# The last tokens' output projection in a two-layer diffusion step: its non-attention half moved into the first score block

## The chip, the cores and the metric

One Trainium2 chip, one core. The metric is the device time of one execution in microseconds (us): the median of three runs of the kernel before is 3267.5 us (3267.45 to 3268.93). TensorE (PE) multiplies, with its weight loads shown apart (PEld); VectorE (DVE), ScalarE (ACT) and GpSimd (POOL) work on tiles; SyncE (SP) issues all the DMAs of this kernel, in program order. Each engine runs its own instructions in order.

## The reference, cut to what matters

```python
D_MODEL, SEQ, DEPTH, DEC_SEQ, PAST_LEN, N_HEADS, N_KV_HEADS = 1024, 256, 2, 2048, 256, 8, 2

def _layer(x, mod, norm_g, w_in, q_g, k_g, conv_w, conv_b, pool_w, pool_scale, w_out, angs, ctx_k, ctx_v):
    shift, scl, gate = jnp.split(mod, 3, axis=-1)
    xn = _rmsnorm(x, norm_g) * (1 + scl) + shift
    proj = xn @ w_in
    q, k, v, z_a, h_c, b_c, c_c, z_c, u_p, z_p = jnp.split(proj, SPLIT_IDX, axis=-1)
    ...                                               # norms and rotary positions of q and k
    attn = _attend(q, k_all, v_all) * jax.nn.silu(z_a)            # channels 0 to 511
    conv = b_c * _short_conv(c_c * h_c, conv_w, conv_b) * jax.nn.silu(z_c)    # 512 to 767
    pool = _pool_mix(u_p, pool_w, pool_scale) * jax.nn.silu(z_p)              # 768 to 1023
    out = jnp.concatenate([attn, conv, pool], axis=-1) @ w_out
    return x + gate * out, k, v
```

It runs for 256 prompt tokens (which attend to themselves) and for 2048 sample tokens (which attend to themselves and to 256 cached keys), in two layers. After the second layer every token is normalized (`_rmsnorm(z, final_g)`). All is float32; the kernel splits each float32 operand of a product into a high and a low part and adds three products (high by high, high by low, low by high).

## The kernel before

Each layer has two phases. Phase A (`phase_a`) normalizes, transposes and multiplies by `w_in`; it writes q, k, v and the gates to DRAM, and the conv and pool channels, already final, as `mH` and `mL` (high and low parts, four chunks of 128 channels). Phase B (`phase_b`) does the attention and the output projection. The order of execution is phase A of layer 0, phase B of layer 0, then the same for layer 1.

Phase B walks over 292 steps. A unit is one head of one block of 512 sample tokens (nine steps of 256 keys), or one pair of prompt heads (one step). Blocks 0 to 3 have eight units each; block 0 also has the four prompt units, one after each of its first four heads. Block 3, the last tokens, takes its heads in the order 4 to 7, 0 to 3 (`h ^ 4 if B.tail`), so that pair 1 ends last. A step s issues on PE the four score products of its 256 keys (`qk`), the value products of a step three earlier (`pv`, LAG = 3), and about two pieces of a coming unit's row maximum (`max_pieces`); ACT takes two exponentials, POOL the low part `pl`, DVE the sums `Z` and the maxima. With a unit's last step come the products of its nine low parts, `fin_a` (adding the two halves), `fin_b`, `fin_b2` (the reciprocal of the sum) and, with the second head of a pair, `fin_c` (c1 to c4: scale, gate on POOL, high part on ACT, low part on POOL), which leaves the pair's tiles in `B.mix`.

The output projection is cut into small functions that wait in a list, `fill`; every step runs one of them (`fill.run`). For blocks 0 to 2 and for the prompt, `outproj` is put there some steps after the block's last pair: 64 functions of six products of 256 columns. In layer 1 the norm of these rows follows, in the list `slow`: `fin_load` reads half a row tile back from DRAM into one of two buffers `oy`, ACT scales it, POOL multiplies by `final_g`, SP writes it out.

Block 3 has no later steps to hide in. Its projection (`outproj_tail`) takes 384 products of 256 columns: per tile of 128 tokens and 256 output columns, 12 for the non-attention channels and 12 for the attention channels. Six of the 16 tiles are begun ahead (`ahead`), the first six functions from five steps before the last step (`el`), the others after the last step; the rest follows in `rest`. Five steps before the end `fill.flush()` empties the list, so that block 2's projection is issued, and `early` loads the conv and pool channels, weights and x. `add` adds products to x and, in layer 1, squares; `finish` takes the root by Newton steps (`newton`, 12 small DVE instructions), scales and writes. `beside` holds the norms of phase A's first two blocks of layer 1, run inside `finish` of layer 0.

Two structures matter for the order: `at(s, f)` puts a function on a step; and a buffer with a fixed count (`bufs`) makes the SP instruction that refills it wait for its last reader, with all that stands behind it on SP.

Of the kernel before, what the change touches and what calls it, by code (L numbers as in the profile page):

```python
# [19 lines left out]
D = 1024  # L20
# [11 lines left out]
PR = {'po': 6, 'q1': 3, 'q2': 5, 's0': 14, 's0p': 7, 'q1p': 2, 'ma': 3, 'mb': 1, 'd0': 3, 'd1': 2, 'dp': 1,  # L32
# [63 lines left out]
def hybrid_step(ctx: ExitStack, tc: tile.TileContext, A, O):  # L96
# [45 lines left out]
    xP2 = scratch("xP2", [NP, D], F32)  # L142

# [889 lines left out]
    def phase_b(l, xs_src, xp_src, xs_dst, xp_dst, nxt):  # L1033
# [3 lines left out]
        with ExitStack() as st, ExitStack() as left:  # L1037
# [6 lines left out]
            def kv_tiles(prompt):  # L1044
                if prompt:
                    t = wk.tile([128, 4, 512], F32R, tag="cl", name="kvp", bufs=1)
                    for g in range(2):
                        for a, v in zip(kvs[True], (t[:, g, 0:256], t[0:65, g, 256:512], t[:, 2 + g, 0:128]
                                                    .bitcast(F16).rearrange("p (t e) -> p t e", e=128))):
                            a.append(v)  # L1050
                    return
# [155 lines left out]
            def zsum(u, grp, ns):  # L1207
# [4 lines left out]
                def one(i):  # L1212
# [48 lines left out]
            def fin_b(u, bc):  # L1261
                ps = pmx.tile([128, 4, 2], F32, tag="mx", name="lc")
                for q in range(4):
                    for i, z in enumerate(u.z2 if u.fh else u.z):
                        nc.tensor.matmul(out=ps[:, q, :], lhsT=z[:, q * 128:(q + 1) * 128], rhs=vones_h if u.fh else vones, start=(i == 0),
                                         stop=(i == u.fh))
# [13 lines left out]
            def fin_c(zs, o, bc, B, pair):  # L1280

                n = B.n
                st = {}

# [6 lines left out]
                def c2():  # L1291
                    padd(o[:, 0:n], o[:, 0:n], zs[:, 0:n], ALU.mult)
# [17 lines left out]
            def outproj(B):  # L1310
# [68 lines left out]
                if last:  # L1379
# [38 lines left out]
                    for t in range(nt):  # L1418
# [6 lines left out]

            def outproj_tail(B):


                rows = [slice(B.t0 + t * 128, B.t0 + (t + 1) * 128) for t in range(4)]
# [3 lines left out]
                def load_x(t, tag, n, bufs):  # L1433
                    xs[t] = []
                    for i in range(0, D, n):
                        x = wk.tile([128, n], F32, tag=tag, name="ox", bufs=bufs)
                        nc.sync.dma_start(out=x, in_=xs_src[rows[t], i:i + n])
                        xs[t] += [x[:, k:k + 512] for k in range(0, n, 512)]

                def load_w(c, part, tile, k0):  # L1440

                    n = tile.shape[1]
                    load(tile, (woH, woL)[part][l][0][:, k0:k0 + n, c * 256:(c + 1) * 256])
                    for k in range(n):
                        ws[c, part, k0 + k] = tile[:, k, :]

                def early():
                    state["c"] = []
                    for i, (tag, m) in enumerate((("ch", mH), ("cl", mL))):
                        t = wk.tile([128, 4, 512], F32R, tag=tag, name=tag, bufs=1)  # L1450
                        load(t, m[:, :, B.t0:B.t0 + 512])
                        state["c"].append(t)
                        for k0 in (4, 0):
                            load_w(1 + i, 1 - i, wk.tile([128, 4, 256], F32R, tag="wo", name="wo", bufs=4), k0)
                    load_x(0, "ox", D, 2)
# [297 lines left out]
```

## Time and profile before

| | |
|---|---|
| median of three runs | 3267.5 us |
| the profiled execution | 3276.25 us, span 3274.5 us |
| phase B, steps 0 to 291 | 709 to 1599 us in layer 0, 2288 to 3200 us in layer 1 |
| PE busy | 3091.0 us, 94% |
| DVE, POOL, ACT busy | 2305.9, 2042.5, 1836.5 us |

A busy time is the share in which the profile shows an instruction running. PE's products overlap, so the distance from one start to the next tells what a product costs, not its length. PEclk is the granted clock of PE as a share of full speed: 1.0 is 2.4 GHz, 0.5 is 1.2 GHz. In the timelines a line has the start in us, the length in us, the engine, the line, the operation, out<-in, shape and count (runs of the same instruction are merged); in brackets the idle time of the engine before it and what ended it.

### The profile page before, as it was taken

How to read it: one execution, taken by the hardware profiler on the slowest of the kernel's cores; microseconds unless marked ns; L12 is line 12 of the kernel's file. 1: busy time of each engine (PE TensorE's matmuls, PEld its weight loads, DVE VectorE, ACT ScalarE, POOL GpSimd, SP SyncE). 2: the span in 40 equal slices, each digit the busy share in tenths (PEclk: the TensorE clock that was granted, in tenths of full speed). 3: DMA queues.
4: the chain of work that ended last, by engine and by line, in shares of the span. 5: the costliest groups of instructions: out<-in, count | busy, mean ns of one | idle time of the engine just before them, and what ended most of it. 6: DMA issues, size and time to landing. Idle time of an engine off the chain costs nothing. (4 is left out here: it accounts for less than half of the span.)

```text
span 3274.5 us, 48199 instructions
## 1 busy us (share of the span) xinstructions
PE 3091.0 (94%) x17818; PEld 2450.8 (75%) x17818; DVE 2305.9 (70%) x3720; ACT 1836.5 (56%) x2638; POOL 2042.5 (62%) x1312
## 2 busy tenths in 40 slices
PE   7899999998999999999999999999899999999997
PEld 5788888765677777767789877987557776676776
DVE  5655575368888888888568546834888888788774
ACT  3223342148877777777533224322888777787772
POOL 2424363238888888887543344521788888798884
PEclk9999999999999999999999999999999999999998
DMA  7245744361341323143633454433323424243335
GB/s 245 74 141 184 246 136 136 117 156 31 94 150 54 103 78 103 52 127 95 207 118 97 142 188 164 144 101 95 73 70 115 127 76 135 64 133 89 102 125 199
DMA packets 367011, 400.02 MB, mean 122 GB/s; under 512 B 31028, under 2 KB 317240, under 8 KB 366008
## 3 DMA queue, kind: packets, MB, share of 16 engines
q1 hardware_dynamic: 366776, 396.94, 39.3%
q8 instruction: 142, 2.33, 0.3%
q14 instruction: 93, 0.76, 0.1%
HBM read 281.50 MB, written 115.36 MB: 121 GB/s over the span
## 5 line engine op out<-in xcount | busy, mean ns | idle before, releaser
L180 POOL TENSOR_TENSOR pl<-P,ph 128x1024 f16<-128x1024 f32 (+2 forms) x594 | 1235.1, 2090 | 277.7 <-ACT ph L1197 260.7
L1147 DVE TENSOR_REDUCE mr<-mx 128x1 f32<-128x512 f32 x1024 | 695.4, 685 | 292.3 <-PE mx L1146 287.1
L1195 ACT ACTIVATE P<-st 128x1024 f32<-128x1024 f32 x576 | 636.6, 1105 | 295.5 <-PE st L1186 287.3
L1217 DVE TENSOR_REDUCE Z<-P 128x152 f32<-128x912 f32 (+2 forms) x576 | 696.1, 1209 | 6.6 <-ACT P L1195 5.5
L1197 ACT ACTIVATE ph<-st 128x1024 f16<-128x1024 f32 x584 | 592.3, 1014 | 0.0
L1146 PE MATMUL mx<-KH,T 128*128 128x512 f32 x1024 | 488.0, 478 | 34.5 <-DVE mr L1147 21.7
L634 PE MATMUL rest<-xh,wh 128*128 128x512 f32 (+1 forms) x1264 | 479.0, 379 | 12.3 <-ACT wh L425 8.6
L636 PE MATMUL rest<-xh,wl 128*128 128x512 f32 (+1 forms) x1264 | 470.0, 372 | 6.2 <-DVE wl L427 4.4
L635 PE MATMUL rest<-xl,wh 128*128 128x512 f32 (+1 forms) x1264 | 469.9, 372 | 0.0
L1185 PE MATMUL st<-T,KH 128*128 128x512 f32 x1152 | 462.8, 402 | 3.1 <-ACT ph L1197 3.1
L1186 PE MATMUL st<-T,KL 65*128 65x512 f32 x1152 | 460.5, 400 | 0.0
L1231 PE MATMUL pv<-ph,V 128*128 128x512 f16 x1152 | 353.9, 389 | 7.7 <-ACT P L1195 4.5
L1146 PEld LDWEIGHTS mx<-KH,T 128*128 128x128 f32 x1024 | 195.7, 191 | 195.3 <-DVE mr L1147 87.1
L634 PEld LDWEIGHTS rest<-xh,wh 128*128 128x128 f32 x1264 | 242.1, 192 | 55.9 <-ACT wh L425 8.8
L427 POOL TENSOR_TENSOR wl<-wf,wh 128x512 fp32r<-128x512 f32 x88 | 124.6, 1416 | 254.5 <-ACT wh L425 230.6
L636 PEld LDWEIGHTS rest<-xh,wl 128*128 128x128 f32 x1264 | 241.5, 191 | 48.7 <-DVE wl L427 5.7
L635 PEld LDWEIGHTS rest<-xl,wh 128*128 128x128 f32 x1264 | 242.2, 192 | 36.9
L1186 PEld LDWEIGHTS st<-T,KL 65*128 65x128 f32 x1152 | 219.4, 190 | 48.1
L1185 PEld LDWEIGHTS st<-T,KH 128*128 128x128 f32 x1152 | 220.1, 191 | 42.8 <-ACT ph L1197 6.1
L475 PE MATMUL qkv<-wl,xh 128*128 128x256 f32 x864 | 247.1, 286 | 4.3 <-DVE wl L427 2.8
L474 PE MATMUL qkv<-wh,xh 128*128 128x256 f32 x864 | 250.9, 290 | 0.0
L476 PE MATMUL qkv<-wh,xl 128*128 128x256 f32 x864 | 246.3, 285 | 0.0
(241 smaller groups left out, 5638.8 us busy)
## 6 DMA issues: line engine op xcount, KB each, us to landing
wo<-woH SPq DMA_DIRECT2D x68, 512.0 KB
wo<-woL SPq DMA_DIRECT2D x68, 512.0 KB
wf<-in_w_in SPq DMA_DIRECT2D x50, 512.0 KB
wa<-in_w_ada SPq DMA_DIRECT2D x24, 1024.0 KB
wf<-in_w_in SPq DMA_DIRECT2D x19, 1024.0 KB
woH<-wgh SPq DMA_DIRECT2D x64, 256.0 KB
woL<-wgl SPq DMA_DIRECT2D x64, 256.0 KB
T<-qH SPq DMA_DIRECT2D x128, 128.0 KB
```

The costliest lines, as they stand in the source:

```text
L180: nc.gpsimd.tensor_tensor(out=out, in0=a, in1=b, op=op)
L634: nc.tensor.matmul(out=ps[:, 0:b.n], lhsT=wh[:, k, ms], rhs=b.h[:, k, :], start=(k == 0), stop=False)
L635: nc.tensor.matmul(out=ps[:, 0:b.n], lhsT=wh[:, k, ms], rhs=b.l[:, k, :], start=False, stop=False)
L636: nc.tensor.matmul(out=ps[:, 0:b.n], lhsT=wl[:, k, ms], rhs=b.h[:, k, :], start=False, stop=(k == KD - 1))
L1146: nc.tensor.matmul(out=ps, lhsT=u.T1[:, q * 128:(q + 1) * 128], rhs=u.KH[u.g][:, c * 512:(c + 1) * 512])
L1147: nc.vector.reduce_max(out=mr[:, q, c:c + 1], in_=ps, axis=AX.X)
L1185: nc.tensor.matmul(out=ps[:, i, :], lhsT=u.KH[u.g][:, kt], rhs=u.T1, start=True, stop=False)
L1186: nc.tensor.matmul(out=ps[:, i, :], lhsT=u.KL[u.g][0:65, kt], rhs=u.T2, start=False, stop=True)
L1195: nc.scalar.activation(out=P, in_=ps, func=AF.Exp, scale=0.125)
L1197: nc.scalar.activation(out=ph, in_=ps, func=AF.Exp, scale=0.125)
L1217: nc.vector.tensor_reduce(out=z[:, c], in_=u.P[grp][:, 0:ns, c, :].rearrange("p s n t -> p n s t"), axis=AX.XY, op=ALU.add)
L1231: nc.tensor.matmul(out=u.po, lhsT=u.V[u.g][:, 2 * j + i, :], rhs=ph[:, i, :], start=(j == 0 and i == 0), stop=False)
```

## The change

In each layer:

- At step 6 a new function list, `outproj_ahead`, is put into `fill` for block 3's tokens: the 192 products of the non-attention channels, in 32 functions of six products, with loads of `mH`, `mL`, weights and x, the sum x + products being written to a new DRAM tensor `xT`. It stands in block 0, where `fill` was empty until the prompt's projection.
- `outproj_tail` keeps the attention channels alone, 96 products of 512 columns, one PSUM tile of 1024 columns per row tile. Five half tiles of them take pairs 2, 3 and 0 in `ahead`, one function per step from the last step on; pair 1 and all else is in `rest`.
- The tail's weights go to `KH1`, `KL1` (22 and 16 steps before the end) and `ch`, `cl` (5 steps before); x comes from `xT`, tiles 2 and 3 ten steps before the end, tiles 0 and 1 five steps before.
- For the last pair, c2 and c4 run on DVE in place of POOL, and the last sum of `Z` is no longer added on POOL: `fin_b` takes two `Z` tiles (twice the small products).
- In layer 1, block 2's rows are read back whole, into the four `wo` tiles, five steps before the end (`late_loads`), and scaled and multiplied as whole rows (`late`). The tail's rows 0 and 1 share one Newton root; the product with `final_g` of half of each row is on DVE (`scalar_tensor_tensor`), the other half on POOL.
- The loop ends as soon as nothing is pending, and phase A's first loads of layer 1 are then issued ahead of `rest`. `fill` runs one function at a time in the tail.
- The prompt's tiles `kvp` and `Pp` get space of their own (one `Pp` buffer, not one of four `wo`).

```diff
-                    t = wk.tile([128, 4, 512], F32R, tag="cl", name="kvp", bufs=1)
+                    t = kvp.tile([128, 2, 640], F32R, tag="kvp", name="kvp")
-                    u.P[0] = wk.tile([128, 1, 512, 2], F32, tag="wo", name="Pp", bufs=4)
+                    u.P[0] = wk.tile([128, 1, 512, 2], F32, tag="Pp", name="Pp", bufs=1)
-                        if grp and (u.blk or grp == 1 or not PR['zl']):
+                        if grp and not (u is units[-1] and grp == u.nst // GRP - 1):
                             padd(z, z, u.z.pop())
+                sub = dsub if B.tail and pair == 1 else padd
...
-                    padd(lo[:, 0:n], o[:, 0:n], h[:, 0:n], ALU.subtract)
+                    sub(lo[:, 0:n], o[:, 0:n], h[:, 0:n], ALU.subtract)
...
+                    def late_loads():
+                        for t in range(nt):
+                            y = wk.tile([128, D], F32, tag="wo", name="oy", bufs=4)
+                            state["y", t] = y
+                            nc.sync.dma_start(out=y, in_=dst[r0:r0 + 128, :])
+                    def late(t, part):
+                        if part == 0:
+                            nc.scalar.mul(out=y, in_=y, mul=state["r"][:, t:t + 1])
+                        else:
+                            padd(y, y, fg, ALU.mult)
+                            nc.sync.dma_start(out=out[r0:r0 + 128, :], in_=y)
...
+            def outproj_ahead(B):
+                def load_c(c):
+                    for w in (woH, woL):
+                        t = wk.tile([128, 4, 256], F32R, tag="wo", name="wo", bufs=4)
+                        load(t, w[l][0][:, 4:8, cs])
+                    x = wk.tile([128, 4, 256], F32, tag="ox", name="ox", bufs=2)
+                    nc.sync.dma_start(out=x, in_=xs_src[rows, cs].rearrange("(t p) n -> p t n", p=128))
+                def start():
+                    for tag, m in (("ch", mH), ("cl", mL)):
+                        load(t, m[:, :, rows])
+                    load_c(0)
+                def mm(c, t, q):
+                    if (t, q) == (0, 1) and c < 3:
+                        load_c(c + 1)
...
+                    if q:
+                        nc.vector.tensor_tensor(out=x[:, t], in0=x[:, t], in1=ps, op=ALU.add)
+                        if t == 3:
+                            nc.sync.dma_start(out=xT[l][:, c * 256:(c + 1) * 256].rearrange("(t p) n -> p t n", p=128),
+                                              in_=x)
+                return ([start, lambda: None, lambda: None]
+                        + [lambda c=c, t=t, q=q: mm(c, t, q) for c in range(4) for t in range(4) for q in range(2)])
...
+                def end():
+                    for part in range(2):
+                        load_w(1, part)
+                    for t in range(2):
+                        xs[t] = wk.tile([128, D], F32, tag="ox", name="ox", bufs=2)
+                        nc.sync.dma_start(out=xs[t], in_=xT[l][t * 128:(t + 1) * 128, :])
...
+                def add(t):
+                    for a, p in ([(x, ps[t])] if t in ps else [(x[:, c], ps[t, c]) for c in range(2)]):
+                        nc.vector.tensor_tensor(out=a, in0=a, in1=p, op=ALU.add)
+                    if last:
+                        for c in range(2):
+                            nc.scalar.activation(out=j, in_=x[:, c], func=AF.Square, accum_out=state["ss"][:, t, c:c + 1])
+                        padd(x[:, 1], x[:, 1], fg[:, 512:1024], ALU.mult)
+                def finish(ts):
+                        r = newton(sm, s, e - a, "or", EPS)
+                    for t in ts:
+                            nc.vector.scalar_tensor_tensor(out=x[:, 0:512], in0=x[:, 0:512], scalar=rt, in1=fg[:, 0:512],
+                                                           op0=ALU.mult, op1=ALU.mult)
+                            nc.scalar.mul(out=x[:, 512:1024], in_=x[:, 512:1024], mul=rt)
+                        nc.sync.dma_start(out=y[B.t0 + t * 128:B.t0 + (t + 1) * 128, :], in_=x)
+                    if beside and ts[-1]:
                         beside.pop(0)()
+                ahead = [lambda: mm(2, 0, (2, 3, 0)), lambda: mm(0, 0, (2, 3, 0)), lambda: mm(0, 1, (2, 3, 0)),
+                         *[lambda c=c, k=k: mm(1, c, (k,)) for c in range(2) for k in (2, 3, 0)]]
+                rest = [lambda: mm(0, 0, (1,)), lambda: mm(0, 1, (1,)), lambda: add(0),
+                        lambda: mm(1, 0, (1,)), lambda: mm(1, 1, (1,)), lambda: add(1), lambda: finish((0, 1)),
+                        lambda: mm(2, 0, (1,)), lambda: mm(2, 1, (2, 3, 0, 1)), lambda: add(2), lambda: finish((2,)),
+                        lambda: mm(3, 0, (2, 3, 0, 1)), lambda: mm(3, 1, (2, 3, 0, 1)), lambda: add(3), lambda: finish((3,))]
+            at(PR['oa'], lambda: fill.add(outproj_ahead(B)))
...
                     fill.flush()
-                    tail[0]()
-                    fill.add([lambda: None] * PR['gap'] + tail[5][:6])
+                    tail[1]()
+                    if last:
+                        before_last.loads()
+                if s >= NSTEP and not (pvq or zq or soon or todo or first):
+                    break
+                if s >= NSTEP - 1 and tail[2]:
+                    fill.add([tail[2].pop(0)])
...
-                nf = 2 if NSTEP - 60 < s < NSTEP and s % PR['fx'] == 0 or s >= NSTEP + 3 else 1
+                nf = 2 if NSTEP - 60 < s < NSTEP and s % PR['fx'] == 0 else 1
...
                 left.close()
-                tail[7].extend(next(nxt))
+                tail[4].extend(next(nxt))
+            fill.add(tail[2] + tail[3])
             while fill.q:
-                fill.run(2)
-                due += 2 * rate
+                fill.run()
+                due += rate
```

## Rows read from the trace of the kernel before

**Rows 1.** The page: busy time of each engine, share of the span, instructions.
```profile
PE 3091.0 (94%) x17818; PEld 2450.8 (75%) x17818; DVE 2305.9 (70%) x3720; ACT 1836.5 (56%) x2638; POOL 2042.5 (62%) x1312
```

**Rows 2.** Stretches: block 0 of both layers, block 1 of layer 0, both tails.
```profile
core 0: us, PE busy (x) PEld busy (x) DVE busy (x) ACT busy (x) POOL busy (x), PEclk, DMA share, GB/s
732.00:833.00 101.00, 87.37 (x421) 53.36 (x420) 83.06 (x118) 82.61 (x117) 82.21 (x47) 0.98 0.19 56
2310.00:2414.00 104.00, 91.87 (x423) 57.09 (x423) 84.30 (x119) 82.70 (x117) 82.37 (x47) 0.94 0.20 60
1012.00:1104.00 92.00, 90.63 (x522) 69.53 (x521) 77.59 (x109) 70.28 (x85) 77.05 (x42) 1.00 0.32 92
...
1598.00:1657.00 59.00, 55.68 (x437) 51.66 (x436) 23.19 (x54) 13.64 (x23) 10.10 (x10) 0.94 0.73 256
3199.00:3257.00 58.00, 54.35 (x426) 50.47 (x424) 23.11 (x56) 13.98 (x26) 26.50 (x34) 0.94 0.62 213
```

**Rows 3.** Timeline of PE: products of 256 and of 512 columns, back to back.
```profile
3216.08 0.28 PE L1493 MATMUL op<-wt,ch 128*128 128x256 f32 x1
3216.20 0.28 PE L1494 MATMUL op<-wt,ch 128*128 128x256 f32 x1
...
3102.40 0.40 PE L1186 MATMUL st<-T,KL 65*128 65x512 f32 x1
3102.64 0.40 PE L1185 MATMUL st<-T,KH 128*128 128x512 f32 x1
```

**Rows 4.** Timeline of the last head of layer 1, from its last score product.
```profile
3199.10 0.61 PE L1231 MATMUL pv<-ph,V 128*128 128x512 f16 x2
...
3204.75 0.58 PE L1495 MATMUL op<-wt,cl 128*128 128x256 f32 x1 [3.65 <-DMA cl<-mL]
...
3206.78 3.70 PE L1238 MATMUL pv<-pl,V 128*64 128x512 f16 x18
...
3212.67 0.95 PE L1265 MATMUL lc<-vones,Z 128*128 128x2 f32 x8
...
3217.53 0.69 DVE L1289 TENSOR_TENSOR o<-o,rlb 128x512 f32<-128x512 f32 x1 [3.69 <-PE rlb L1288]
...
3220.32 1.29 POOL L180 TENSOR_TENSOR mixl<-o,mixh 128x512 fp32r<-128x512 f32 x1 [0.30 <-ACT mixh L1296]
```

**Rows 5.** Timeline of layer 0's end: last head, phase A's loads, squares, norms.
```profile
1619.25 1.29 POOL L180 TENSOR_TENSOR mixl<-o,mixh 128x512 fp32r<-128x512 f32 x1 [0.73 <-ACT mixh L1296]
...
1626.95 4.00 SPq L299 DMA_DIRECT2D x<-xS  x8
...
1630.79 1.06 ACT L312 ACTIVATE junk<-x 128x1024 bf16<-128x1024 f32 x1 [11.62 <-DMA x<-xS]
...
1635.87 0.17 DVE L316 TENSOR_SCALAR ms<-ss 128x4 f32<-128x4 f32 x1 [2.17 <-ACT junk L312]
...
1638.47 2.74 DVE L323 TENSOR_SCALAR x<-x,nt_y 128x1024 f32<-128x1024 f32 x4
...
1656.73 1.52 DVE L441 TENSOR_SCALAR xf<-trx,modA,modB 128x512 f32<-128x512 f32 x2
```

**Rows 6.** Waits of 3199 to 3274 us: engine, line, releaser, us in total, times, longest.
```profile
ACT oy L1412 <- DMA oy<-xS: 12.8, 4, 5.3
```

**Rows 7.** Timeline of layer 1's end: a Newton step beside POOL, adds, squares, last scaling.
```profile
3256.90 1.26 POOL L180 TENSOR_TENSOR ox<-ox,fg 128x512 f32<-128x512 f32 x1
3256.99 1.18 DVE L151 TENSOR_TENSOR nt_t<-nt_t,nt_v 128x1 f32<-128x1 f32 x1
...
3260.04 1.28 DVE L1502 TENSOR_TENSOR ox<-ox,op 128x512 f32<-128x512 f32 x2
...
3265.49 0.63 ACT L1505 ACTIVATE oj<-ox 128x512 bf16<-128x512 f32 x1
3266.03 0.19 ACT L1505 ACTIVATION_READ_ACCUMULATOR oj<-ox 128x1 f32 x1
...
3270.15 0.72 ACT L1519 ACTIVATE ox<-ox,nt_y 128x512 f32<-128x512 f32 x1 [3.94 <-DVE nt_y L152]
```

More of the change, by code (lines that the diff above doesn't have):

```diff
@@ L142, in hybrid_step @@
     xP2 = scratch("xP2", [NP, D], F32)
+    xT = [scratch(f"xT{l}", [512, D], F32) for l in range(DEPTH)]
     def newton_parts(pool, src, n, tag, eps):
@@ L1426, in outproj_tail @@
             def outproj_tail(B):
-                rows = [slice(B.t0 + t * 128, B.t0 + (t + 1) * 128) for t in range(4)]
+                rows = slice(B.t0, B.t0 + B.n)
                 beside = []
                 xs, ws, ps, state = {}, {}, {}, {}
[L1433 to L1455, printed above, removed]
+                def load_w(c2, part):
+                    if c2:
+                        w = wk.tile([128, 4, 512], F32R, tag=("ch", "cl")[part], name="wt", bufs=1)
+                    else:
+                        w = kvp.tile([128, 4, 512], F32R, tag=("KH1", "KL1")[part], name="wt")
+                    load(w, (woH, woL)[part][l][0][:, 0:4, c2 * 512:(c2 + 1) * 512])
+                    ws[c2, part] = w
@@ L1497, in add @@
-                def add(t, c2):
-                    x = xs[t][c2]
-                    xv = x.rearrange("p (a n) -> p a n", a=2)
-                    c = 2 * c2
-                    for o, p in ([(xv, ps[t, c, 2])] if (t, c, 2) in ps else [(xv[:, i], ps[t, c + i]) for i in range(2)]):
-                        nc.vector.tensor_tensor(out=o, in0=o, in1=p, op=ALU.add)
-                    if last:
-                        j = wk.tile([128, 512], mybir.dt.bfloat16, tag="og", name="oj", bufs=1)
-                        nc.scalar.activation(out=j, in_=x, func=AF.Square, accum_out=state["ss"][:, t, c2:c2 + 1])
@@ L1509, in finish @@
+                def finish(ts):
+                    a, e = ts[0], ts[-1] + 1
+                    y = O["y_sample"][0] if last else xs_dst
                     if last:
-                        s = sm.tile([128, 1], F32, tag="os", name="os")
-                        nc.vector.tensor_reduce(out=s, in_=state["ss"][:, t, 0:2], axis=AX.X, op=ALU.add)
+                        s = sm.tile([128, 2], F32, tag="os", name="os")[:, 0:e - a]
+                        nc.vector.tensor_reduce(out=s, in_=state["ss"][:, a:e, :], axis=AX.X, op=ALU.add)
@@ L1523, in finish @@
-                    if beside:
-                        beside.pop(0)()
-                n2 = PR['a2']
-                ahead = [lambda t=t, c=c, q=q: mm(t, c, q) for t, c in PR['ao'] for q in (2, 0, 1)]
-                rest = []
-                for t in range(4):
-                    for c in range(4):
-                        rest += [lambda t=t, c=c, q=q: mm(t, c, q) for q in ((2, 0, 1, 3) if 4 * t + c >= 4 + n2 else (3,))]
-                        if c % 2:
-                            rest.append(lambda t=t, c=c: add(t, c // 2))
-                    rest.append(lambda t=t: finish(t))
@@ L1538, in phase_b @@
+                return half, end, ahead, rest, beside
             units = []
@@ L1540, in phase_b @@
             prompt_B = Blk()
-            prompt_B.prompt, prompt_B.n, prompt_B.t0, prompt_B.mix, prompt_B.tail = True, NP, 0, {}, False
+            prompt_B.prompt, prompt_B.n, prompt_B.t0, prompt_B.mix, prompt_B.tail, prompt_B.late = True, NP, 0, {}, False, False
             def add_unit(prompt, blk, h, B):
@@ L1551, in phase_b @@
                 B = Blk()
-                B.prompt, B.n, B.t0, B.mix, B.tail = False, 512, blk * 512, {}, blk == 3
+                B.prompt, B.n, B.t0, B.mix, B.tail, B.late = False, 512, blk * 512, {}, blk == 3, blk == 2
+                before_last = B if blk == 2 else None if blk < 2 else before_last
                 for h in range(8):
```

128 lines of the change are left out of this document (63 added, 65 removed), and 6 rows, old and new, of the table PR.

## The prediction

> **What bounds the kernel now.** I read the page first: PE is busy for 94% of the span, the others for 56 to 70% [rows 1]. So a gain must come from a place where PE waits, or where it works while something else could be done beside it. The busy time by stretches finds two such places [rows 2]. In block 0, between the first heads and the prompt's projection, PE is busy for 87.4 of 101 us in layer 0 and 91.9 of 104 us in layer 1, while in block 1, with a projection among the steps, it is busy for 90.6 of 92 us. And in the tails, the 58 to 59 us behind the last score product, PE is busy nearly all the time, but DVE, ACT and POOL for 10 to 27 us each: nothing is left there to hide the projection beside. The timeline of PE then gives the price of a product, from start to start: 0.12 us at 256 columns, 0.24 us at 512 [rows 3]. The timelines of the last head and of the two ends show what comes last [rows 4, 5, 7], and the waits what the final norm stands for [rows 6].
>
> **Moved: the non-attention products.** 192 products of 0.12 us are 23.0 us of PE per layer, out of the tail and into 32 steps of block 0. What they cost there is not shown by any row, so I bound it. If nothing is hidden it is 23.0 us a layer. If PE's idle time there is used first (13.6 and 12.1 us [rows 2]) it is 9.4 and 10.9 us. If the stretch comes to run like block 1, which passes 522 products in 92.0 us, 0.176 us each, then 421 + 192 = 613 take 108.0 us and 615 take 108.4 us: 7.0 and 4.4 us more. The low end is zero: PE's clock, at 0.98 and 0.94 there and at 1.00 in block 1 [rows 2], would give back at most 2 and 6 us if it stayed up. I take 7.0 and 4.4, since block 1 is the same kind of step with the same kind of filling: 11.4 us. DVE gets 16 adds of half the 0.69 us that 512 columns take [rows 4], some 6 us on 83 us of 101: beside PE.
>
> The moved step's DMAs count too. At step 6 SP issues 2 loads of 1 MB, 2 of 0.5 MB and x of 0.5 MB, 3.5 MB just ahead of head 4's keys. The stretches give 295 to 350 GB/s at a full DMA share (56 at 0.19, 256 at 0.73 [rows 2]), so 10 to 12 us, and the first product stands three steps of 3.2 us later: a wait of 0.4 to 2.4 us. The q loads of the next prompt unit come behind these and the keys, and PE's maxima wait for them; the later loads of 1.5 MB per 256 columns have seven steps. I put 1 us a layer on this, 0 to 10. Each store to `xT` makes SP wait for the last add of its column, with the next heads' q loads behind; these are asked for many steps ahead. Block 0 together: 13.4 us for both layers.
>
> The `Pp` buffer that falls from four to one is reused ten steps later, and `kvp` leaves `cl`: no cost.
>
> **The last head.** Before, from the last score product (3199.10) PE waited 3.65 us for `cl`, then ran its low parts at half clock until 3210.48 (3206.78 + 3.70), and `mixl`, the last tile of pair 1, ended at 3221.61 [rows 4]. After, three half tiles of nine products stand in front of the low parts: 27 x 0.236 = 6.4 us, with six value products (1.4 us) and 18 low parts at full clock (half of 3.70, 1.85 us): 3208.8. `cl`, now a weight, is loaded second and not fourth, and is wanted at about 3204: no wait, or a short one. From there to `mixl` it was 11.1 us; c2 and c4 on DVE at 0.69 and not 1.29 us take 1.2 off, the sums' products double (+0.95), and the products that stand between on PE's queue shrink from about 2.2 to 1.4 us and from 2.9 to 1.4 us: 11.1 - 1.2 + 0.95 - 0.8 - 1.5 = 8.6 us. `mixl` ends at 3217.4, 4.2 us earlier. The dropped POOL add of `Z` is not on this path.
>
> **What is left for PE behind it** is 51 products of 512 columns, 12.0 us: PE ends at 3229.4 in layer 1 (before 3257) and, with the same 4.2 us off 1620.54 [rows 5], at 1628.3 in layer 0. Neither is the end of its stage; other engines are late next.
>
> **Layer 0: phase A's norms.** Before, the first x loads were issued behind two stores, at 1626.95, and phase A's first tile came out of its transposes at 1656.73 [rows 5]. After, the loads are issued when the loop ends, as soon as the key tiles under them are free, by about 1612. ACT squares a row tile every 1.27 us (four from 1630.79 to 1635.87), from 1616 on: the first block's are done at 1621, the second's at 1626. DVE must then do, in order: Newton 2.6 us (1635.87 to 1638.47) and scaling 2.74 us for block one, to 1626.5; the third tile's add of 1.28 us [rows 7], 1627.8; Newton and scaling for block two, 1633.1; the last add, 1634.4. Then the first transposed tile: 1656.7 - 1634.4 = 22.3 us gained. At best PE sets it (28 us); if the loads come only with PE's end, 8 us.
>
> **Layer 1: three rounds of the final norm.** The rows of block 2, read through two buffers, made ACT wait 12.8 us [rows 6]; now they are there beforehand. What is left is a chain through DVE and ACT, for rows 0 and 1, then 2, then 3: add 1.3 us, two squares 1.6 us (0.63 + 0.19 each), Newton, scaling of two halves 1.0 us [rows 7]. Newton is 2.6 us alone, but its step took 1.18 us where POOL multiplied beside it [rows 7], 1.0 us more; with two such steps it is 4.6 us, the round 8.5 us. The first begins with row 1's add, at 3217.4 + 12 products (2.8 us) + 0.3 = 3220.5; one whole row of block 2 on ACT (twice 0.72 us) stands in it. 3220.5 + 25.5 + 1.4 = 3247.4, and from the last scaling's end (3270.87) to the span's end it was 3.6 us: 3251.0, 23.5 us gained. With PE as the bound it is 3229.4 + 1.3 + 1.6 + 2.6 + 0.7 + 3.6 = 3239.2, 35 us.
>
> **The sum** is 23.5 + 22.3 - 13.4 = 32.4 us of the profiled execution's 3276.25 us, or 0.99%. The median of the runs is 8.75 us shorter; 0.99% of it gives 3235.2 us, so 3235.
>
> **The rivals.** (a) Block 0 hides nothing: 2 x 24 us for 45.8 us gained, 3270 us. For it: ACT, DVE and POOL are each busy for 82% of that stretch, so its steps of 3.2 us may not be PE's alone. Against it: block 1 has the same load on them and steps of 3.0 us. (b) Slower: SP and DMA in block 0. Each of the four loads of 1.5 MB and more (5 us at 300 GB/s) stands in front of q loads that PE's maxima need; if PE waits it out every time, that is 20 us a layer on top of 23 unhidden, 3267.5 - 45.8 + 86 = 3308 us. It decides from 26 us a layer on. Against it: DMA's share is 0.19 to 0.20 there. (c) Phase A's loads come late, 8 and not 22.3 us: 3249 us. (d) DVE held by POOL at the end. POOL now multiplies whole rows, so a held step could cost twice the 1.26 us: two or three of them in each round, 7.5 us more, 3243 us. The Trainium skill's page "SBUF — State Buffer", section "Who interferes with whom", says that a VectorE instruction with two SBUF inputs and a GpSimd instruction that reads SBUF block each other, the second for the whole of the first; by that rule moving c2, c4 and the product with `final_g` to DVE speaks against the change. The 1.18 us step [rows 7] agrees. (e) All covers hold: block 0 costs 4 us, the tails give 26 and 31 us: 3214 us. (f) The change does not do what it says, `ahead` standing in front of the last head's products and not beside a wait: that is in the sum already, as 6.4 us.
>
> **How the numbers follow.** Forecast 51% (its own range 3222 to 3250), (d) 14%, (e) 13%, (c) 10%, (a) 8%, (b) 4%. The range leaves out (a), (b) and the lower half of (e), some 18%: 3213 to 3259. A measurement can tell about 0.2% from no change, 6.5 us: faster is below 3261, the forecast, (c), (d) and (e) and a little of (a), 0.89; within it 0.07, most of (a); slower 0.04, (b).
>
> **What would show it.** In block 0, 32 steps of about 3.3 us (105 to 109 us in the two stretches) with PE busy above 95% and no wait for `ch`, `cl` or q longer than 2 us: else (a) or (b). In the tail, low parts ending near 10 us behind the last score product, and no half clock; `mixl` 18 us behind it; PE's last product 30 us behind it, where it was 58. In layer 0, x loads before the first x store, and the first `xf` 36 us behind the last score product, released by DVE's add and not by PE. In layer 1 no wait for `oy` on ACT, and an end 52 us behind the last score product, with three Newton rounds as the chain. The forecast is wrong if block 0 takes over 20 us more per layer, or if a load is last in either tail.

## The result, and the profile after

The median of the changed kernel's first five runs is 3249.05 us (3240.66 to 3256.75), beside 3268.93 us of the kernel before: a ratio of 0.9938 (0.9914 to 0.9962), some 20 us or 0.6% less. The forecast was 3235 us; the time lies in its range, at the upper end of the likeliest case's own (3222 to 3250). The profiled execution took 3245.29 us (span 3243.3), 31 us less than the profiled one of before. That pair flatters the change by 11 us; where those 11 us are is the main question of the runs.

The page's line of engines, answering [rows 1]:

```profile
PE 3071.8 (95%) x17642; PEld 2437.3 (75%) x17642; DVE 2325.7 (72%) x3734; ACT 1834.6 (57%) x2634; POOL 2031.7 (63%) x1298
```

Stretches, as in [rows 2]: block 0 of layer 0, block 1, layer 0's end up to phase A, and layer 1's end, cut where PE ends (us; busy time and count of PE, PEld, DVE, ACT, POOL; granted clock; DMA share; GB/s):

```profile
727.00:837.30 110.30, 105.70 (x607) 78.35 (x605) 88.35 (x133) 82.10 (x116) 80.97 (x47) 0.98 0.42 107
...
1012.00:1104.00 92.00, 90.58 (x523) 69.73 (x521) 77.37 (x109) 69.32 (x87) 74.98 (x40) 1.00 0.32 92
1610.00:1645.00 35.00, 30.30 (x158) 22.99 (x156) 23.57 (x51) 13.50 (x22) 6.30 (x7) 1.00 0.64 238
...
3190.00:3221.00 31.00, 28.77 (x145) 21.43 (x143) 17.69 (x21) 9.10 (x16) 15.72 (x23) 1.00 0.33 130
3221.00:3243.00 22.00, 0.00 (x0) 0.00 (x0) 14.35 (x45) 7.63 (x14) 7.13 (x4) 0.52 0.42 167
```

PE now ends 22 us ahead of the span's end, and its clock falls only behind it; up to then it was granted in full, where [rows 2] have 0.94. Block 0 is longer, block 1 is as it was.

For the account I take two traces of before (the one shown, and a second one, below) and three of the changed kernel (the first, its repeat, and the control with 128 idle products, below). The marks are the starts of ACT's exponentials of steps 0, 42 and 291 in each layer, of the last score product and of the first `xf` of phase A, and the span's end. Means in us:

| stretch | before | after | difference | forecast |
|---|---|---|---|---|
| start to step 0, layer 0 | 709.1 | 705.0 | -4.1 | 0 |
| steps 0 to 42, layer 0 | 128.0 | 138.3 | +10.3 | +8.0 |
| steps 42 to 291, layer 0 | 760.5 | 768.6 | +8.1 | 0 |
| last score product to first `xf` | 57.9 | 35.2 | -22.7 | -22.3 |
| first `xf` to step 0, layer 1 | 630.2 | 624.3 | -5.9 | 0 |
| steps 0 to 42, layer 1 | 129.1 | 140.3 | +11.2 | +5.4 |
| steps 42 to 291, layer 1 | 780.8 | 781.8 | +1.0 | 0 |
| last score product to the end | 75.6 | 53.6 | -22.0 | -23.5 |

The sum is -24 us; without the first row, which lies before any edit could act except one in phase A and which varies from 703 to 709 us in the traces of either kernel, -20, as the medians have it. A row is good to a few us: in all nine traces with these products steps 0 to 42 take 137.4 to 144.4 us in layer 0 and 137.4 to 142.5 in layer 1, where PE's clock was granted at half (0.5, 1.2 GHz) for 3 to 17 us of them (more of that with the experiments). The two ends came out as forecast. Block 0 costs 21.5 and not 13.4 us, and two stretches that the forecast left alone moved: layer 0's later blocks, and phase A of layer 1.

### The profile page after: what moved, and what is told of

It reads as the page before. It is cut to its first block, busy times and chain, and to the rows that moved or that the text cites. A ratio compares the mean times of both kernels' runs of the same rounds, so it can differ in the third digit from the quotient of the medians.

```text
span 3243.3 us, 47832 instructions
## 1 busy us (share of the span) xinstructions
PE 3071.8 (95%) x17642; PEld 2437.3 (75%) x17642; DVE 2325.7 (72%) x3734; ACT 1834.6 (57%) x2634; POOL 2031.7 (63%) x1298
## 6 DMA issues: line engine op xcount, KB each, us to landing
T<-qH SPq DMA_DIRECT2D x128, 128.0 KB
```

## The steps of the forecast in the trace

The last head of layer 1, timelines of PE and DVE, answering [rows 4]; the last score product ends here at 3189.85:

```profile
3197.45 2.13 PE L1239 MATMUL pv<-pl,V 128*64 128x512 f16 x18
...
3207.38 0.69 DVE L184 TENSOR_TENSOR mixl<-o,mixh 128x512 fp32r<-128x512 f32 x1 [0.68 <-ACT mixh L1299]
...
3219.14 0.39 PE L1542 MATMUL op<-wt,mixl 128*128 128x512 f32 x1
```

Low parts done 9.7 us behind it (forecast 10), `mixl` 18.2 (18), PE's last product 29.7 (30), the end 53.4 (52). The 3.65 us wait for `cl` is gone, and the 18 low parts take 2.13 and not 3.70 us.

The end of layer 0, timelines of SP, ACT and DVE, answering [rows 5]; the last score product ends at 1610.1:

```profile
1610.04 15.99 SPq L300 DMA_DIRECT2D x<-xS  x8
...
1626.96 0.62 ACT L1299 CAST mixh<-o 128x512 fp32r<-128x512 f32 x1 [3.22 <-DVE o L184]
1627.48 1.05 ACT L313 ACTIVATE junk<-x 128x1024 bf16<-128x1024 f32 x1
...
1641.23 2.74 DVE L324 TENSOR_SCALAR x<-x,nt_y 128x1024 f32<-128x1024 f32 x4
1643.89 1.22 DVE L1547 TENSOR_TENSOR ox<-ox,op 128x1024 f32<-128x1024 f32 x1
1645.02 1.53 DVE L442 TENSOR_SCALAR xf<-trx,modA,modB 128x512 f32<-128x512 f32 x2
```

The first `xf` comes 34.9 us behind (forecast 36), right behind DVE's last add, and PE waits for it. The forecast's times are those of the trace of before, where the last score product ends 12 us earlier, at 1598.1. Measured from that product the chain ran as forecast: the last five of the eight loads are issued 13.7 to 15.5 us behind it (forecast about 14; the first three go at once, the five wait for the last head's small tiles), the squares begin 17.4 us behind it (18), DVE's second scaling ends at 33.9 (35) and its last add at 35.0 (36). The squares stand on ACT right behind `mixh`, which the forecast does not say; the time is the same.

The three rounds of layer 1, timelines of DVE and POOL, answering [rows 6, 7] (ACT's wait for `oy` is gone from the waits):

```profile
3214.89 2.41 POOL L181 TENSOR_TENSOR oy<-oy,fg 128x1024 f32<-128x1024 f32 x1 [1.26 <-ACT oy L1433]
...
3216.41 0.92 DVE L1560 TENSOR_SCALAR os<-os 128x2 f32<-128x2 f32 x1
3217.25 1.29 POOL L181 TENSOR_TENSOR ox<-ox,fg 128x512 f32<-128x512 f32 x1
3217.36 1.21 DVE L154 TENSOR_SCALAR nt_v<-os 128x2 f32<-128x2 f32 x1
3218.49 2.37 POOL L181 TENSOR_TENSOR oy<-oy,fg 128x1024 f32<-128x1024 f32 x1
3218.60 2.28 DVE L155 TENSOR_SCALAR nt_t<-nt_v 128x2 int32<-128x2 int32 x1
...
3225.34 2.35 POOL L181 TENSOR_TENSOR oy<-oy,fg 128x1024 f32<-128x1024 f32 x1 [4.48 <-ACT oy L1433]
...
3226.85 0.15 DVE L1560 TENSOR_SCALAR os<-os 128x1 f32<-128x1 f32 x1
...
3227.64 1.26 POOL L181 TENSOR_TENSOR ox<-ox,fg 128x512 f32<-128x512 f32 x1
3227.79 1.13 DVE L152 TENSOR_TENSOR nt_t<-nt_t,nt_v 128x1 f32<-128x1 f32 x1
3228.86 2.34 POOL L181 TENSOR_TENSOR oy<-oy,fg 128x1024 f32<-128x1024 f32 x1
3228.96 2.26 DVE L153 SCALAR_TENSOR_TENSOR nt_y<-nt_t,nt_y 128x1 f32<-128x1 f32 x1
3231.26 0.16 DVE L151 SCALAR_TENSOR_TENSOR nt_t<-nt_y 128x1 f32<-128x1 f32 x1
```

A small step of DVE takes 0.16 us alone; beside a product of POOL most take 0.9 to 2.3 us and end when POOL's product ends, and some, as the one at 3226.85, are not held (the last section has which). The rounds took 6.6, 5.7 and 2.9 us. The forecast had 4.6 for each, 13.8 for 15.2; rival (d) is there, but only 1.4 us beyond the price I had put on it.

## Experiments

**The changed kernel again** (no edit) and **the kernel before again** (no edit).

> The changed kernel once more, unedited, to see what in its time is the change and what is the single execution. Theory: the stretches that the change edits come out as in its first profile to within 2 us (block 0 of layer 0 about 10.8 us and of layer 1 about 8.0 us longer than in the kernel before; each tail about 22 us shorter), and what differs between two executions lies in the stretches between, which the change doesn't touch; the median is again between 3240 and 3257 us, 0.4 to 0.9% faster than the kernel before. Rival: the first profile was a lucky execution, and block 0 or a tail is 8 us or more longer in this one.

> The kernel before once more, unedited, for a second trace. Its profiled execution stands 6 to 9 us above the median of its runs, and the two profiled executions differ by 31 us where the medians differ by 20. Theory (chance of single executions): in this one the unedited stretches (phase A of layer 0, blocks 1 to 3) are together 5 to 10 us shorter than in the first, while block 0 takes again 127 to 130 us for its first 42 steps and the last stage 74 to 75 us from the last exponential's start. Rival: one of the edited stretches is itself several us shorter than in the first trace, so that the change gains less there than the first pair of traces shows.

Measured: 3250.58 us (3248.11 to 3256.81), ratio 0.9939 (0.9924 to 0.9953), and 3266.2 us for the one run of before. The second trace of before is 10.1 us shorter than the first; of that 3.4 us lie behind layer 0's last exponential, 6.6 us in blocks 1 to 3 of both layers. Its block 0 takes 128.4 and 128.6 us, its last stage 74.73 (first trace: 74.74). The changed kernel's last stage is 52.73 us from that mark (52.77). So the last stage repeats within 0.05 us, and the 31 us of the first pair were 20 us of change and 11 us of single executions. The granted clock accounts for the 10.1 us between the two traces of before (span, and mean granted clock as a share of full speed):

```profile
core 0: 3274.5 us, clock 0.980
...
core 0: 3264.4 us, clock 0.983
```

A share of 0.020 of 3274.5 us is 65 us, and 0.017 of 3264.4 us is 55 us: 10 us, by an estimate that takes all of PE's lost clock as lost time. One expectation failed: layer 1's block 0 was to repeat within 2 us and took 142.4 us for 137.4. In steps 0 to 42 there PE's clock was granted at half for 17 us, and for 6.8 us in the first trace, which is 5 us by the same estimate. But layer 0's blocks 1 to 3 took 667.7 and 668.2 us in the two traces of the changed kernel, 660.7 and 657.7 in those of before: a gap of 7 us or more, where two traces of one kernel differ by 3 at most.

**Few products ahead; nothing ahead.** The first keeps 2 of 12 products of each tile with all loads, adds and stores; the second drops the list and reads x from its source.

```diff
-                    for k in (2 * q, 2 * q + 1):
-                        nc.tensor.matmul(out=ps, lhsT=mh, rhs=wht[:, k, :], start=(k == 0), stop=False)
...
+                    if q == 0:
+                        nc.tensor.matmul(out=ps, lhsT=mh, rhs=wht[:, q, :], start=True, stop=False)
+                    else:
+                        nc.tensor.matmul(out=ps, lhsT=ml, rhs=wlt[:, q, :], start=False, stop=True)
```

```diff
-            at(PR['oa'], lambda: fill.add(outproj_ahead(B)))
...
-                        nc.sync.dma_start(out=xs[t], in_=xT[l][t * 128:(t + 1) * 128, :])
+                        nc.sync.dma_start(out=xs[t], in_=xs_src[B.t0 + t * 128:B.t0 + (t + 1) * 128, :])
```

> The changed kernel with 2 instead of 12 products per tile ahead (32 and not 192 a layer; the other 160 are left out, so the last rows' projection is incomplete), all loads, adds and stores kept. Theory (PE's steps of block 0 take up about half of the products): of 160 x 0.12 = 19.2 us a layer some 8 us come back, 16 us in all. Rival 1, the products cost nothing and what block 0 lost is waits for DMA and SP: under 5 us come back. Rival 2, nothing is hidden: 38 us come back.

> The changed kernel without the products ahead, their loads, adds and stores; the tail reads x itself (the non-attention channels of the last rows are left out). Theory: block 0 runs as in the kernel before, 10.8 and 8.0 us faster, 19 us in all, of which all but 2 to 4 us is already back in the run with few products. Rival (SP and DMA): 8 us or more beyond the run with few products. The tails stay as they are, within 1 us.

Measured: 3233.5 us (17 below the change) and 3219.74 us (31 below). The first is the number expected, but by chance; the second is not: 14 us between them where I expected 2 to 4. The medians can't be read as prices of block 0. Steps far behind it moved as well (the section on layer 0's later blocks), so that of the 17 us only 10 lie in steps 0 to 42 of both layers. And the clock blurs these stretches: with few products it was granted at half for 20 us of layer 0's steps 0 to 42, with nothing ahead for 31 us of layer 1's (135.8 us, where 129 were expected), in the changed kernel for 7 to 17 us. What block 0 pays is plain where the clock was full, in steps 20 to 29 of layer 0, ten steps with ten functions (stretches of before, after and few products):

```profile
765.50:798.10 32.60, 27.45 (x136) 17.06 (x134) 27.02 (x39) 26.48 (x40) 26.26 (x15) 1.00 0.12 33
```

```profile
763.40:798.70 35.30, 33.18 (x194) 24.62 (x193) 28.26 (x44) 26.00 (x39) 25.94 (x16) 1.00 0.35 101
```

```profile
766.00:799.00 33.00, 29.25 (x149) 19.08 (x147) 29.16 (x45) 26.26 (x38) 25.95 (x15) 1.00 0.44 132
```

By the exponentials' starts the ten steps take 32.6 us before, 35.8 after, 33.3 with few products and 32.6 with nothing ahead. Sixty products of 0.12 us are 7.2 us, and 3.1 of them show, 44%; 32 functions make 10.0 us, about what each layer's block 0 lost (10.3 and 11.2). PE's idle time falls from 5.2 to 2.1 us and not to nothing. Fifty of the sixty products cost 2.4 us; the loads, the adds and the other ten 0.7. So in these steps SP and DMA, rival (b), are at most a small part of it (over steps 0 to 42 of both layers, in the three traces of the changed kernel, PE waits for a load 0.5 us at the longest): it is PE, and somewhat over half of the products are hidden.

**No whole-row products of POOL in the last stage.**

```diff
-                            padd(y, y, fg, ALU.mult)
                             nc.sync.dma_start(out=out[r0:r0 + 128, :], in_=y)
```

> The changed kernel with POOL's four whole-row products by final_g in the last stage left out (block 2's rows go out without final_g), everything else kept. Theory (DVE's 128x1 steps are held while POOL multiplies): of the held steps those beside whole rows go (0.92, 2.28 and 2.26 us for 0.16 each), about 5 us; the Newton rounds fall from 6.6 and 5.7 us to about 4 us each, and the end comes 48 us and not 53.4 us behind the last score product. Rival (the rounds wait for ACT or PE anyway, or the long steps are something else): under 1 us.

Measured: the last stage takes 47.03 us from layer 1's last exponential where it was 52.75, 5.7 us less (expected 5); the rounds are 3.8, 2.9 and 2.9 us. Of the held steps these are left, beside the half-row products (timeline of DVE):

```profile
3209.52 1.17 DVE L1559 TENSOR_SCALAR os<-os 128x2 f32<-128x2 f32 x1
...
3217.81 0.39 DVE L151 SCALAR_TENSOR_TENSOR nt_t<-nt_y 128x1 f32<-128x1 f32 x1
```

The median is 3239.44 us, 11 us below the change; 5.7 of these are the stage's, the other 5 were not followed up (single runs of one kernel spread by up to 16 us).

**The last stage in two rounds.** Block 2's rows go to DVE, two of them while row 1's squares run; rows 2 and 3 share a root.

```diff
-                        if part == 0:
-                            nc.scalar.mul(out=y, in_=y, mul=state["r"][:, t:t + 1])
-                        else:
-                            padd(y, y, fg, ALU.mult)
+                        nc.vector.scalar_tensor_tensor(out=y, in0=y, scalar=state["r"][:, t:t + 1], in1=fg,
+                                                       op0=ALU.mult, op1=ALU.mult)
...
+                    rest = rest[:6] + late[:2] + rest[6:10] + rest[11:13] + late[2:3] + rest[13:14] + late[3:] + [lambda: finish((2, 3))]
```

> The changed kernel with the last stage rebuilt so that no whole-row product of POOL falls into it: block 2's four rows are scaled and multiplied on DVE in one step each (about 1.4 us), two while row 1's squares run, and rows 2 and 3 share one Newton round. Theory: the held steps go (5 us, as without the products) and a round of some 3 us plus its wait of 1.7 us, against four DVE steps of 1.4 us, of which about half lie in waits: the end comes about 46 us behind the last score product and not 53.4 us, 7 us gained in the end. Rival (DVE becomes the bound, as it takes over 5.6 us of POOL's work): no better than 52 us.

Measured: 44.50 us from that mark, 8.25 us less (expected 7); 3237.72 us, ratio 0.9893 (0.9877 to 0.991), 12 us below the change, of which 8 are the stage's. The rival's 52 us did not come.

**Phase A's loads behind the first two stores.**

```diff
             if nxt:
+                fill.add(tail[2] + tail[3][:7])
+                fill.flush()
                 left.close()
                 tail[4].extend(next(nxt))
-            fill.add(tail[2] + tail[3])
+                fill.add(tail[3][7:])
```

> One part undone: phase A's eight x loads at the end of layer 0 stand behind the first two x stores on SP again, and the norms of its two blocks come one round later. Theory: with the loads early the squares began 17.4 us behind the last score product, because ACT's queue held them behind the last head's cast, so of the early loads only some 9 us are used; behind the stores, from about 22 us on, they begin near 26 us, and layer 0's end becomes 8 to 10 us longer. The forecast's own price for late loads was 14 us (22.3 less 8). Rival (PE sets this stage): under 2 us.

Measured: the squares begin 27.0 us behind the end of the last score product, and now for want of data (timeline of ACT):

```profile
1644.60 1.06 ACT L313 ACTIVATE junk<-x 128x1024 bf16<-128x1024 f32 x1 [9.47 <-DMA x<-xS]
```

The first `xf` comes 43.9 and not 35.2 us behind that product's start, 8.7 us later (expected 8 to 10), and layer 1 begins 6.6 us later; 3259.23 us. The part holds; loads and norms move together in it, and no run separates them. The 14 us that the expectation compares with are not tested here: they were for loads that come with PE's end, 30 us behind the last score product, and here the first is issued 22.5 us behind it.

**Block 2's rows in halves through two buffers** (`B.late` false, loads in the old order).

> One part undone: block 2's rows are again read back in halves through two buffers, in their old order among the steps, and not as whole rows ahead of the end. Theory: ACT waits for these loads again (12.8 us before), but the chain of the last stage goes through DVE's Newton rounds, and ACT's halves stand in them only in part: the end comes 2 to 8 us later than 53.4 us. Rival 1: the whole wait is on the chain, 12 us or more. Rival 2: the smaller products of POOL hold DVE less, and the end is the same or earlier.

Measured: 54.75 us, 2.0 us more (expected 2 to 8); 3255.93 us. ACT waits again, 5.1 and 4.3 us at the longest, but mostly beside DVE's rounds. So of the 22 us of layer 1's end this part is 2, though its wait was 12.8 us [rows 6].

**Why layer 0's later blocks were longer.** With the products ahead, steps 211, 263 and 275 (blocks 2 and 3) took 5 to 9.5 us longer together, behind waits for weights that are loaded in the same order, at the same distance, as before. What differs is a packet on another DMA queue. The queues in the 8 us ahead of step 211 (queue, packets, MB, share of 16 engines), and PE's waits for these weights over blocks 1 to 3 (total, times, longest), in the changed kernel:

```profile
q1 hardware_dynamic: 1830, 1.95, 82.1%
q8 instruction: 1, 0.02, 1.0%
...
PE op L1362 <- DMA wo<-woL: 9.3, 7, 2.4
```

In the kernel before there is no such packet in these 8 us, and the waits are shorter:

```profile
q1 hardware_dynamic: 1807, 1.92, 82.4%
...
PE op L1359 <- DMA wo<-woL: 4.6, 5, 1.6
```

The waits are not all of it. Step 275 of the changed kernel is 4.2 us longer than the shortest; PE waits 2.45 us in it, and 1 us behind this wait its clock is granted at half (0.50, 1.2 GHz) for 3.4 us, while the low parts run (timeline of PE, and the stretch):

```profile
1561.87 0.39 PE L1362 MATMUL op<-wo,ch 128*128 128x256 f32 x1 [2.45 <-DMA wo<-woL]
...
1562.90:1566.30 3.40, 3.40 (x18) 1.31 (x18) 0.00 (x0) 0.00 (x0) 0.41 (x1) 0.50 1.05 355
```

So of the 9.5 us in this trace 6.0 are waits (1.8, 1.7 and 2.45), and two stretches of 3.4 us at half clock are the rest. In the trace without POOL's whole-row products the waits are 5.0 us, the clock stays full behind them, and the three steps are 5.0 us longer.

Over the whole execution the page of the changed kernel has, for this queue:

```profile
q8 instruction: 140, 2.29, 0.3%
```

These are 140 packets of 16 KB, for 17642 products and as many weight loads: 252 instructions of PE to a packet, and 257 with its 691 semaphore and drain instructions (the packets start 256 of these apart in the mean). So these are PE's instructions being fetched, and 192 products more ahead of a step move the fetches behind it by 384 instructions, one and a half periods. The Trainium skill's page "Runtime: NRT & Kernel Launch", section "Instruction fetch mechanics", says that the instruction memory is refilled in 16 KiB blocks of 256 instructions over a DMA queue of its own, and that the cost of crossing a block is mostly hidden. The trace agrees on the block; whether it is hidden, the next runs tell. They add products of two columns behind the first transposes, where PE waits for its first weights; nobody reads them.

```diff
+        idle = ptr.tile([2, 2], F32, tag="tr", name="idle")
+        for _ in range(64):
+            nc.tensor.matmul(out=idle, lhsT=vones_h, rhs=vones_h)
```

> The changed kernel with 64 products of two columns added behind the first transposes, where PE waits 9 us for its first weights; nobody reads them, and they take nothing later. They move PE's instructions by 128: the traces show one 16 KB fetch on the instruction queue per 256 instructions of PE, so every later fetch comes half a period earlier in the work. In all six runs with the products ahead, layer 0's blocks 1 to 3 took 663 to 670 us, and steps 211, 263 and 275 waited 5 to 9.5 us together for the projection's weights, with a fetch some 3 us ahead of the wait, between the weights' packets; in the four runs without them (before, few, none) 657 to 663 us and 0.6 to 1.7 us. Theory (the fetches' place): the three steps wait under 2 us again, layer 0's blocks 1 to 3 take 657 to 661 us, and the median falls by 5 to 8 us; other places may win or lose a wait. Rival (the new scratch tensor, or what block 0 leaves behind): nothing moves.

> The control: 128 such products, a whole period of the fetches. Theory: the same places as in the changed kernel, steps 211, 263 and 275 wait 5 to 9.5 us together, layer 0's blocks 1 to 3 take 663 to 670 us, the time is that of the changed kernel within 5 us. Rival (added products at the start change the rest in some other way): as with 64.

> The mirror: the kernel before, with nothing of the change, and 64 such products. Theory: now its fetches stand where those of the changed kernel do in layer 0's blocks 1 to 3; steps 211, 263 and 275 wait 5 to 9.5 us together (0.6 to 1.7 before), these blocks take 663 to 670 us (661 and 658 before), and the median rises by 5 to 8 us. Rival: as before.

Measured (median; steps 42 to 291 of layer 0; what steps 211, 263 and 275 are longer than their shortest in any trace):

| | us | ratio to before | steps 42 to 291 | three steps |
|---|---|---|---|---|
| before, and again | 3268.9 | | 762.0, 759.0 | 1.7, 0.6 |
| before, 64 idle products | 3284.09 | 1.0045 (1.0029 to 1.006) | 769.7 | 9.8 |
| changed, and again | 3249.05, 3250.58 | 0.9938, 0.9939 | 768.9, 769.5 | 9.5, 9.5 |
| changed, 128 idle products | 3252.21 | 0.9946 (0.993 to 0.9961) | 767.5 | 6.0 |
| changed, 64 idle products | 3238.62 | 0.99 (0.9885 to 0.9915) | 759.1 | 1.1 |

With half a period the changed kernel loses these waits, and the kernel before gets them; with a whole period all stays. Both medians moved further than the 5 to 8 us expected, by 12 and 13 us. In all fourteen traces PE waits 1.2 to 2.6 us for `woL` in each of the three steps where a fetch lies 2 to 7 us ahead of the step, between the weights' packets, and 0 to 1.3 us where none does. PE's waits for these weights, in the kernel before with 64 idle products and in the changed one with 64:

```profile
PE op L1362 <- DMA wo<-woL: 9.2, 7, 2.1
PE op L1361 <- DMA wo<-woH: 0.9, 1, 0.9
```

```profile
PE op L1365 <- DMA wo<-woL: 3.5, 5, 1.0
```

So the fetch is not hidden where a load has no slack. With the fetches at like places in these blocks the change gains 32.1 us (3270.76 less 3238.62) or 31.9 us (3284.09 less 3252.21). That the packet delays the load on the one DMA engine that both use is what the rows suggest; no run separates it from other ways in which the fetch could hinder it. The kernel before lost 13 us and not only the 9 of these steps: its trace is also 5 us longer in phase A of layer 1 and 5 us in that layer's steps 42 to 291; whether its fetches met other loads there was not followed up.

**Both together**, two rounds and 64 idle products:

> Both together: the last stage in two rounds, and 64 products at the start. Theory: the two gains add up, 3237.7 less 5 to 8, some 3231 us, ahead of both kernels. Rival: the moved fetches meet other loads, and nothing is left of it.

Measured: 3232.4 us (3223.56 to 3239.14), ratio 0.9884 (0.9866 to 0.9901), as expected; it beats both kernels, the change by 17 to 20 us. By the 12 us that the shift alone was worth it would have been 3226 us, so the gains do not quite add up, as far as six runs that spread by 16 us can tell.

## Why the prediction was right, and where it was not

**The ends: right.** 22.7 and 22.0 us for 22.3 and 23.5. Every mark of the last head came within 0.5 us, and those of layer 0's norms within 1.5 us. These chains were summed from rows of the same instructions, one after another, and the instructions ran again as in those rows. In layer 1 the chain is the forecast's too, but the held steps were 1.4 us more than its sum had.

**Block 0: the right mechanism, mis-sized.** The term was 7.0 and 4.4 us, from "block 1 is the same kind of step": 0.176 us for a product. The stretch came to 110.3 us and 607 products, 0.182 us: 10.3 and 11.2 us a layer, where I had 8.0 and 5.4 with 1 us each for the queue. That 1 us is not in the traces, where PE's longest wait for a load in block 0 is 0.5 us. In layer 1 block 1's rate also stood for a clock of 1.00, where the rows of before have 0.94; but in the three traces of the changed kernel PE's clock was still granted at half for 7 to 17 us of steps 0 to 42 there, as for 10 to 17 us in those of before. What stays is 2 us of PE's idle time in ten steps, in three waits for DVE and ACT that the new products, which stand elsewhere on PE's queue, do not fill (timeline of PE in the changed kernel, from 763.4 to 798.7):

```profile
774.75 1.05 PE L1267 MATMUL lc<-vones,Z 128*128 128x2 f32 x8 [0.43 <-DVE mr L1148]
...
792.95 0.47 PE L1176 MATMUL mxb<-dg,ones_r 128*128 128x512 f32 x1 [0.61 <-ACT mixh L1299]
...
797.42 0.50 PE L1147 MATMUL mx<-KH,T 128*128 128x512 f32 x1 [0.89 <-ACT T L1177]
```

Rival (a), nothing hidden, was further off on the other side (48 us for 21.5).

**Left out: where PE's instructions are fetched.** "Moved" I read as work and loads; the instructions themselves are moved as well, and their fetches met the projection's weights two blocks later: 8 us, in waits and in the lower clock behind them, that stand in no term, in no rival and in no edited stretch.

**Left out: a number in the change.** The list `PR` has `'po': 4` in place of 6, which neither the list of edits nor the prediction speaks of. It makes phase A issue the pooled channels' last products two functions earlier and so changes SP's order there. Before, the waits of phase A in layer 1 and SP's queue have:

```profile
PE rest L634 <- ACT wh L425: 8.6, 1, 8.6
...
1872.50 9.68 SPq L772 DMA_DIRECT2D gate<-gateD  x2
1882.28 1.01 SPq L411 DMA_DIRECT2D wf<-in_w_in  x2
1883.34 2.85 SPq L173 DMA_DIRECT2D mHp<-mh  x1
```

and after:

```profile
1850.59 0.32 SPq L174 DMA_DIRECT2D mHp<-mh  x1
...
1862.92 1.28 SPq L773 DMA_DIRECT2D gate<-gateD  x2
1864.25 1.05 SPq L412 DMA_DIRECT2D wf<-in_w_in  x2
```

`wf` stood behind a `gate` load that waited 9 us for a buffer; PE waited 8.6 us for `wf`, in all three traces of before and in none of the changed kernel, where the longest wait is 5.1 us. This is the 5.9 us gained between the first `xf` and layer 1. The order on SP follows from the code and is seen; that this number alone makes the gain was not tried by a run.

The two omissions nearly cancel (8.1 and 5.9 us), which is luck. So the forecast missed by 12 us: 8 us of block 0, 2 us of these two, 2 us of the ends and of layer 1's later steps.

## What to carry to other kernels

Work that is moved beside other work isn't free where the engine seems idle: take a stretch of ten steps and see how much of the idle time is waits that the new work can't use; here a little over half of the products was hidden. A time that moved in a stretch that no edit touches may be the granted clock of one execution, so take a second trace of both kernels; what repeats is a finding, and one looks there for what has shifted (the fetches of instructions among the loads, the order on a queue). And read every changed constant in the diff: one of them is the likely source of 6 us here.

## What the runs showed of the hardware

- Where a fetch of 16 KB of PE's instructions, one per 256 of them, fell among the packets of loads that had no slack, PE waited 1.2 to 2.6 us for these loads (0 to 1.3 us without it), and behind some of the waits its clock was granted at half for 3.4 or 6.8 us. Half a period of shift was worth 12 us in one kernel and 13 us in the other.
- Two traces of one kernel differ by the granted clock: 0.980 and 0.983 of full speed go with the 10 us between the two of before.
- DVE steps of 128x1 and 128x2, among them `tensor_scalar` with one input, took 0.9 to 2.3 us beside POOL's products and 0.16 alone. It goes both ways: with block 2's rows on DVE, two half-row products of POOL took 4.37 us together, for 1.26 to 1.29 each. The Trainium skill's page "SBUF — State Buffer", section "Who interferes with whom", names for such a lock instructions with two SBUF inputs and those in a two-port mode, `tensor_scalar` among the latter; the trace agrees.
- Some steps beside a running product of POOL were not held (DVE's five at 3226.66 to 3227.56, beside 3225.34 to 3227.69). Which ones, the fourteen traces show, counted over DVE's steps of 1 to 4 columns that begin 0.4 us or more before the end of a POOL product of over 1 us: all 100 `tensor_scalar` steps of 128x1 ran in 0.16 us, and no reciprocal and no reduction of up to 20 columns was held either; all `tensor_tensor` and `scalar_tensor_tensor` steps of any of these widths and all `tensor_scalar` steps of 128x2 and 128x4 were held to the end (323 of 330; of the other seven five began within 6 ns of POOL's own start, and two read PSUM). So a root for two rows is held at its `tensor_scalar` steps too, and a root for one row only at the steps with two tensors.
